# One PSUM bank moved from plain products to attention scores in a two-layer hybrid decoder

## Chip, cores and metric

The kernel runs on one core of one Trainium2 chip. The metric is the device time of one execution in microseconds (us), lower is better. Before the change three runs took 1982.52, 1983.05 and 1984.99 us; their median is 1983.05 us.

## What is computed

x has 512 tokens of 1024 channels in float32. Two layers run one after the other, each of this form (shortened from the reference):

```python
h = rms_norm(x, mix_norm_g[l])
proj = h @ w_in[l]                       # split into the inputs of three mixers and three gates
ya = nsa_mixer(...)      # compressed blocks, selected blocks, window: 8 heads of 64
yb = mla_mixer(...)      # latent attention: 8 heads, 96 wide keys, 64 wide values
yc = rglru_mixer(...)    # causal conv, gated linear recurrence, GeLU gate
merged = sigmoid(ma) * (ya @ w_pa[l]) + sigmoid(mb) * (yb @ w_pb[l]) + sigmoid(mc) * (yc @ w_pc[l])
x = x + merged @ w_o[l]
h = rms_norm(x, ffn_norm_g[l])
x = x + (silu(h @ ffn_w1[l]) * (h @ ffn_w3[l])) @ ffn_w2[l]
```

In `nsa_mixer` the compressed branch first makes one key and one value for every block of 32 tokens with a small two-layer network (`cmp_w1`, `cmp_w2`); with 512 tokens the selected branch selects all causal blocks, so both it and the window branch are causal attention.

## The kernel before

**Products.** Every large product is done in two halves per operand: `split` (L99) makes a high part on ScalarE (ACT, L100) and a low part on VectorE (DVE) or GpSimd (POOL) (L101), and `mm3` (L111) issues three matmuls (L113 to L115) per 128 rows of the contraction. A product of 1024 rows and 512 columns (`gemm_gen`, L121) is 24 matmuls into one PSUM tile of 128 x 512 float32, one bank. `block_tm` (L393) fills four banks at once, 24 matmuls each.

**PSUM.** `ps(tag)` (L87) takes a tile from one of four rotating sets of banks: `mm` for plain products, `s` for attention scores, `t` for transposes, `o` for the attention output. A tile's first matmul waits until the last reader of the tile that had its bank before is done. `pbufs` (L76) gives the number of banks of each set; together they are the eight banks. In the dense part (`wide`, L1219 on: the recurrence, the merges, the output product and the feed-forward network) a plain product takes its bank from `mm`, `s` and `t` in the order of the table `WIDE` (L33), seven banks in turn.

**Order.** The program is written in Python order by `layer` (L1078), and a list scheduler then orders the instructions of each engine with its own model of durations and free banks. So what is queued where follows from the banks too. Each engine runs its instructions in that order.

**A layer.** First the products for the compressed branch (`kv`, L1084, two tiles that stay open over eight steps) beside the first token-major block (L1085); then `b_in` (L757: five plain products with an eviction by DVE L339, a scaling by ACT L768 and DVE L769, and a square by ACT L774), of which the second is left open after two of its eight steps while `block3` (L404, evicted by ACT L413, L414, L422 and DVE L423) runs. Inside `block3` the two first stages of the compressed network (`cmp_mlp` L450; 16 small matmuls L461 each, evicted by ACT L465 and DVE L466) are put: the first takes a `t` bank, the second an `mm` bank (L459). Then the second token-major block, and the query and key transposes (`a_qk` L547: PE L544, ACT L551, DVE L550).

The attention (`attn`, L706) is a loop over 24 jobs of three stages each: scores (`st_s` L616: matmuls L748 and L749, or L113 to L115 for the latent heads; DVE L633 masks and finds the minimum in the bank; ACT L636 exponentiates out of the bank, which is then free), normalising (DVE L643, L645), transposes (`st_t` L649: PE L660, ACT L100, DVE L101) and values (`st_v` L666: L673, L674). Between them `fill` (L342) puts steps of plain products: the gate products (`gates_a` L930, evicted by DVE L339), the key-value products of the latent heads (`b_kv` L848: 16 per layer, six matmuls of 256 columns each, evicted by ACT L863, ACT L422 and DVE L423), their queries (`b_halfq` L807, ACT L819) and the first merge (`merge_a` L935, DVE L938).

Of the kernel before, what the change touches and what calls it, by code (L numbers as in the profile page):

```python
# [29 lines left out]
TLAG, VLAG = 6, 2  # L30
EB = 79
F0, F1 = 11.5, 2.5
WIDE = ("s", "t", "mm", "t", "s", "mm", "t")  # L33
YK, YQ = 1.3, 1.5
KB = 2
NLAG = 4, 4
# [27 lines left out]
class Builder:  # L64
    def __init__(self, ctx, tc, io, layers=L, dbg=None):
        self.tc, self.nc, self.io, self.layers = tc, tc.nc, io, layers
        self.dbg = dbg or {}
        nc = self.nc
        self.V, self.A, self.T = nc.vector, nc.scalar, nc.tensor
        pool = lambda n, b=1, **k: ctx.enter_context(tc.tile_pool(name=n, bufs=b, **k))  # L70
        self.cst, self.sb, self.sm = pool("cst"), pool("sb"), pool("sm", 2)
        self.psum = pool("psum", 1, space=PSUM)
        self.n = 0
        self.bufs = dict(wr=3, wh=4, wl=4, h=16, mg=8, oT=8, cq=10, qk=8, v=8, big=6, pt=5, P0=2, P1=2, P2=2, P3=3, e=3)
        self.pending = False
        self.pbufs = dict(mm=2, s=2, t=3, o=1)  # L76
        self.wide, self.turn = False, 0
        self.weng, self.debt, self.mid = None, 0.0, False

# [7 lines left out]
    def ps(self, tag="mm"):  # L87
        if tag == "mm" and self.wide:
            self.turn += 1
            tag = WIDE[self.turn % 7]  # L90
        return self.psum.tile([128, 512], F32, tag=tag, name=self.nm("ps" + tag), bufs=self.pbufs[tag])
# [986 lines left out]
    def layer(self, l):  # L1078
# [2 lines left out]
        self.wide, self.weng, self.peng = False, None, V  # L1081
        self.rows(l)
        self.bg = [self.rope_tables()] if l == 0 else []
        kv = [self.ps(), self.ps()]  # L1084
        for k in self.steps(self.block_tm(io["wb12"][l, 0], N12)):  # L1085
            if k % 4 == 0:
                w = [self.weights(self.win(l, c, 0)[:, k * 128:k * 128 + 512]) for c in ("kc", "vc")]
            s = slice((k % 4) * 128, (k % 4) * 128 + 128)
# [139 lines left out]
        for oc in range(KC):  # L1228
            t = self.pg("mg")
# [95 lines left out]
```

## Time and profile before

| what | us |
|---|---|
| median of three runs | 1983.05 |
| the profiled execution, its own time | 1982.81 |
| its span, first to last instruction | 1981.0 |
| TensorE matmul (PE) busy | 1935.6 |
| VectorE (DVE) busy | 1319.7 |
| ScalarE (ACT) busy | 996.6 |
| GpSimd (POOL) busy | 252.0 |

Layer 0 runs from 0 to about 1000 us, layer 1 from there to the end. In each layer the attention and what feeds it takes about the first 340 us, the dense part the rest. "Busy" is the union of an engine's instructions; for PE the ends are modelled and matmuls overlap, so that the distance from start to start tells a matmul's price better than its length. In a timeline row the bracket at the end is the idle time of the engine just before, and what ended it.

### The profile page before, as it was taken

The page shows a single profiled execution, that of the slowest core. Times are in us where ns is not written, and L with a number is a line of the kernel's source. Part 1 is how long each engine was busy: PE and PEld are TensorE (multiplying, and loading weights), DVE is VectorE, ACT ScalarE, POOL GpSimd, SP SyncE. Part 2 cuts the span into 40 slices and gives each one's busy share as a digit, 9 for nine tenths or more (in the row PEclk, how much of TensorE's full clock was granted, in tenths as well). Part 3 has the DMA queues.
Part 4 walks back from the last instruction along what each step waited for, and adds up shares of the span by engine and source line. Part 5 has one row for each costly group of instructions (what it writes and reads, how often), then busy time and mean ns, then how long its engine had stood idle before and what let it go on. Part 6 is the DMA issues. An engine that isn't in the chain of part 4 may idle for free.

```text
span 1981.0 us, 26967 instructions
## 1 busy us (share of the span) xinstructions
PE 1935.6 (98%) x9472; PEld 1627.8 (82%) x9472; DVE 1319.7 (67%) x2783; ACT 996.6 (50%) x1937; POOL 252.0 (13%) x232
## 2 busy tenths in 40 slices
PE   9898999999999999999999899999999999999999
PEld 8777878888888888888888688888888888888887
DVE  8689998788545554455556999878874465534542
ACT  5466776687334332233344577857773343323331
POOL 0453442000000000000004536310000000000000
PEclk9999999999999999999999999999999999999999
DMA  5211101223333223323432111113233322333333
GB/s 159 86 56 34 41 31 43 87 94 104 109 125 101 96 96 93 99 98 96 131 112 93 43 41 44 38 46 100 95 102 119 121 91 100 96 94 99 97 102 100
DMA packets 100519, 173.94 MB, mean 88 GB/s; under 512 B 11936, under 2 KB 26144, under 8 KB 100384
## 3 DMA queue, kind: packets, MB, share of 16 engines
q1 hardware_dynamic: 100384, 172.22, 27.3%
q8 instruction: 74, 1.21, 0.2%
q14 instruction: 61, 0.50, 0.1%
HBM read 167.98 MB, written 4.19 MB: 87 GB/s over the span
## 4 chain that ended last, share of the span: by engine, by line
PE 78%; DVE 8%; ACT 2%; issue 1%; POOL 0%; ACTq 0%; DVEq 0%; POOLq 0%
PE pst L114 9%; PE pst L113 9%; PE pst L115 9%; PE psmm L113 8%; PE psmm L114 8%; PE psmm L115 8%; PE pss L114 7%; PE pss L113 7%; PE pss L115 7%; PE pst L660 1%; DVE P L645 1%; DVE pss L633 1%; PE pso L673 1%; PE pso L674 1%; ACT P L636 1%
## 5 line engine op out<-in xcount | busy, mean ns | idle before, releaser
L100 ACT ACTIVATE wh<-wr 128x512 fp32r<-128x512 f32 (+3 forms) x640 | 387.5, 608 | 698.4 <-PE pst L114 261.0
L101 DVE TENSOR_TENSOR wl<-wr,wh 128x512 fp32r<-128x512 f32 (+2 forms) x526 | 355.1, 676 | 247.5 <-ACT wh L100 242.4
L101 POOL TENSOR_TENSOR wl<-wr,wh 128x512 fp32r<-128x512 f32 (+2 forms) x114 | 138.8, 1224 | 951.8 <-ACT wh L100 935.8
L113 PE MATMUL psmm<-h,wh 128*128 128x512 f32 x600 | 237.2, 395 | 3.7 <-ACT wh L100 2.8
L115 PE MATMUL psmm<-h,wl 128*128 128x512 f32 x600 | 235.2, 392 | 0.6 <-POOL wl L101 0.6
L114 PE MATMUL psmm<-h,wh 128*128 128x512 f32 x600 | 235.0, 392 | 0.0
L113 PE MATMUL pst<-h,wh 128*128 128x512 f32 x512 | 199.8, 390 | 0.0
L114 PE MATMUL pst<-h,wh 128*128 128x512 f32 x512 | 199.3, 389 | 0.0
L115 PE MATMUL pst<-h,wl 128*128 128x512 f32 x512 | 199.3, 389 | 0.0
L113 PEld LDWEIGHTS psmm<-h,wh 128*128 128x128 f32 x600 | 112.9, 188 | 26.4 <-ACT wh L100 3.2
L113 PE MATMUL pss<-h,wh 128*128 128x512 f32 x344 | 134.2, 390 | 0.0
L115 PE MATMUL pss<-h,wl 128*128 128x512 f32 x344 | 133.9, 389 | 0.0
L114 PE MATMUL pss<-h,wh 128*128 128x512 f32 x344 | 133.9, 389 | 0.0
L115 PEld LDWEIGHTS psmm<-h,wl 128*128 128x128 f32 x600 | 112.9, 188 | 24.6 <-POOL wl L101 1.1
L114 PEld LDWEIGHTS psmm<-h,wh 128*128 128x128 f32 x600 | 112.9, 188 | 20.8
L636 ACT ACTIVATE P<-pss,nm 128x512 f32<-128x512 f32 x192 | 100.1, 525 | 55.4 <-DVE nm L633 32.3
L113 PEld LDWEIGHTS pst<-h,wh 128*128 128x128 f32 x512 | 96.1, 188 | 20.2 <-ACT e L984 0.4
L115 PEld LDWEIGHTS pst<-h,wl 128*128 128x128 f32 x512 | 96.1, 188 | 20.1
L114 PEld LDWEIGHTS pst<-h,wh 128*128 128x128 f32 x512 | 96.1, 188 | 19.8
L633 DVE CUSTOM_DVE_ANT_0 pss<-pss,mask 128x512 f32<-128x512 f32 x192 | 93.7, 489 | 7.2 <-PE pss L115 5.8
L660 PE MATMUL pst<-ident,P 128*128 128x128 f32 x480 | 76.6, 274 | 11.5 <-DVE P L645 5.3
L660 PEld LDWEIGHTS pst<-ident,P 128*128 128x128 f32 x480 | 58.2, 141 | 28.1 <-issue 17.8
(423 smaller groups left out, 4303.4 us busy)
## 6 DMA issues: line engine op xcount, KB each, us to landing
wr<-w SPq DMA_DIRECT2D x240, 256.0 KB, 2.6
wr<-wfm SPq DMA_DIRECT2D x188, 256.0 KB, 2.6
wr<-wpc SPq DMA_DIRECT2D x32, 256.0 KB, 2.6
wr<-wo SPq DMA_DIRECT2D x32, 256.0 KB, 2.6
wr<-wb SPq DMA_DIRECT2D x32, 192.0 KB, 2.4
wr<-w SPq DMA_DIRECT2D x32, 192.0 KB, 2.3
mg<-xT SPq DMA_DIRECT2D x16, 256.0 KB, 2.7
wr<-wpa SPq DMA_DIRECT2D x16, 256.0 KB, 2.6
```

What stands on the lines that cost most here:

```text
L100: self.A.activation(hi, src, AF.Copy)
L101: (eng or self.V).tensor_tensor(lo, src, hi.bitcast(F32), OP.subtract)
L113: mm(ps, a[0], b[0], start=first, stop=False)
L114: mm(ps, a[0], b[1], start=False, stop=False)
L115: mm(ps, a[1], b[0], start=False, stop=last)
L633: self.V.tensor_tensor_reduce(p[:, :W], p[:, :W], self.mask[:, 512 - W:], 1.0, 3e38, OP.add, OP.min, j.nm[:, i:i + 1])
L636: self.A.activation(j.Pi[i], p[:, :128 * (i + 1)], AF.Exp, bias=j.nm[:, i:i + 1], scale=-1.0, accum_out=j.l[:, i:i + 1])
L645: V.tensor_scalar(j.Pi[i], j.Pi[i], j.gate[:, i:i + 1], j.l[:, i:i + 1], op0=OP.mult, op1=OP.mult)
L660: self.T.transpose(ps[:, c:c + 128], j.Pi[i][:, kt * 128:kt * 128 + 128], self.ident)
L673: T.matmul(o[:, 512 - n:], j.V[kt], h[:, m0:m0 + n], start=j.first and kt == 0, stop=False)
L674: T.matmul(o[:, 512 - n:], j.V[kt], l_[:, m0:m0 + n], start=False, stop=j.last and kt == NT - 1)
```

## The change

Three places: the banks become one for plain products, three for scores, three for transposes, one for the output; the table of the dense part visits those seven banks; and the second of the two open tiles at a layer's start comes from the score banks, as one `mm` bank can't hold two open tiles.

```diff
-WIDE = ("s", "t", "mm", "t", "s", "mm", "t")
+WIDE = ("s", "t", "mm", "s", "t", "s", "t")
...
-        self.pbufs = dict(mm=2, s=2, t=3, o=1)
+        self.pbufs = dict(mm=1, s=3, t=3, o=1)
...
-        kv = [self.ps(), self.ps()]
+        kv = [self.ps(), self.ps("s")]
```

No instruction is added or removed; 1464 of PE's 9323 matmuls stand at another place in its order, all of them before the dense parts or in their first steps.

**Place one, the start of layer 1.** On PE, before, the second product of the compressed network (L461 into `psmm_10121`) stands inside `block3`:

```order
L115 MATMUL pss_9970<-wh_10099,h_9463 128x312
L461 MATMUL psmm_10121<-pt_9876,qk_10117 64x62 x8
L461 MATMUL psmm_10121<-pt_9877,qk_10118 64x62 x8
L113 MATMUL pst_9967<-wh_10144,h_9523 128x312
L114 MATMUL pst_9967<-wl_10145,h_9523 128x312
```

Now it stands after the end of the open product of `b_in` (`psmm_9935`), whose bank it has to take over, and the third product of `b_in` (`psmm_10276`) stands behind it:

```order
L113 MATMUL pst_10290<-wh_10294,h_9159 128x384
L114 MATMUL pst_10290<-wl_10295,h_9159 128x384
L461 MATMUL psmm_10121<-pt_9876,qk_10117 64x62 x8
L461 MATMUL psmm_10121<-pt_9877,qk_10118 64x62 x8
L115 MATMUL pst_10290<-wh_10294,h_9160 128x384
L113 MATMUL pss_10291<-wh_10294,h_9159 128x384
L114 MATMUL pss_10291<-wl_10295,h_9159 128x384
L115 MATMUL pss_10291<-wh_10294,h_9160 128x384
L113 MATMUL pss_10292<-wh_10294,h_9159 128x384
L113 MATMUL psmm_10276<-h_9159,wh_10278 128x512
```

So 16 small matmuls moved from the middle of `block3` to a place some 40 matmuls later. On ACT, before, the eviction of that product (L465 from `psmm_10121`) stood ahead of those of `block3`:

```order
L100 ACTIVATE wh_10251<-wr_10250 128x512
L465 ACTIVATE cth_10138<-psmm_10121 64x62
L100 ACTIVATE wh_10278<-wr_10277 128x512
L422 ACTIVATE v_10184<-pst_9967,ny_9775 128x4x64
L422 ACTIVATE v_10189<-pst_9968,ny_9775 128x4x64
```

and now it stands behind the scaling and the square (L768, L774) of the product whose bank it follows:

```order
L100 ACTIVATE wh_10332<-wr_10331 128x384
L768 ACTIVATE cq_10270<-e_10268,vec_6780 128x512
L774 ACTIVATE e_10268<-e_10268 128x512
L465 ACTIVATE cth_10138<-psmm_10121 64x62
L100 ACTIVATE wh_10351<-wr_10350 128x384
```

On DVE L466 moves in the same way, behind the two additions L538. Layer 0 has the same move.

**Place two, the query and key transposes of layer 0.** On PE, before, the first of them (L544) stand inside the product after next:

```order
L113 MATMUL psmm_1185<-h_121,wh_1187 128x512
L114 MATMUL psmm_1185<-h_122,wh_1187 128x512
L115 MATMUL psmm_1185<-h_121,wl_1188 128x512
L544 MATMUL pst_1198<-ident,big_563 128x128 x2
L544 MATMUL pst_1198<-ident,big_564 128x128 x2
```

Now two sets stand at once behind the product `psmm_924`, while its bank is emptied:

```order
L115 MATMUL psmm_924<-h_169,wl_1116 128x512
L544 MATMUL pst_1198<-ident,big_563 128x128 x2
L544 MATMUL pst_1198<-ident,big_564 128x128 x2
L544 MATMUL pst_1233<-ident,big_563 128x128 x2
L544 MATMUL pst_1233<-ident,big_564 128x128 x2
L113 MATMUL psmm_1141<-h_79,wh_1143 128x512
```

The first set moved 30 matmuls of 512 columns ahead.

**Place three, the latent heads' key-value products of layer 0.** On PE, before, between two of them there was other work or a free second bank:

```order
L114 MATMUL psmm_2187<-wl_2142,cq_1252 128x256
L115 MATMUL psmm_2187<-wh_2141,cq_1253 128x256
L544 MATMUL pst_2208<-ident,big_1322 128x128 x2
L113 MATMUL psmm_2197<-wh_2141,cq_1180 128x256
L114 MATMUL psmm_2197<-wl_2142,cq_1180 128x256
```

Now three of them share the one bank with nothing, and with three transposes, between them:

```order
L114 MATMUL psmm_2146<-wl_2142,cq_1252 128x256
L115 MATMUL psmm_2146<-wh_2141,cq_1253 128x256
L113 MATMUL psmm_2187<-wh_2141,cq_1180 128x256
L114 MATMUL psmm_2187<-wl_2142,cq_1180 128x256
L115 MATMUL psmm_2187<-wh_2141,cq_1181 128x256
L113 MATMUL psmm_2187<-wh_2141,cq_1252 128x256
L114 MATMUL psmm_2187<-wl_2142,cq_1252 128x256
L115 MATMUL psmm_2187<-wh_2141,cq_1253 128x256
L660 MATMUL pst_2261<-ident,P_1951 128x128
L660 MATMUL pst_2261<-ident,P_1952 128x128
L660 MATMUL pst_2261<-ident,P_1953 128x128
L113 MATMUL psmm_2197<-wh_2141,cq_1180 128x256
```

Most of the other key-value products have 9 to 16 matmuls of other work between them now.

## Rows read from the trace of the kernel before

**Rows 1.** The page's first lines: span, and PE's busy time, share and instructions.

```profile
span 1981.0 us, 26967 instructions
PE 1935.6 (98%) x9472; PEld 1627.8 (82%) x9472; DVE 1319.7 (67%) x2783; ACT 996.6 (50%) x1937; POOL 252.0 (13%) x232
```

**Rows 2.** Waits of PE, longest in total: engine line, released by: us, times, longest.

```profile
PE pss L748 <- ACT P L636: 10.6, 13, 1.4
PE pst L660 <- DVE P L645: 5.3, 3, 2.7
```

**Rows 3.** Busy us by stretch: length, PE, PEld, DVE, ACT, POOL, granted clock, DMA.

```profile
65.00:85.00 20.00, 12.98 (x56) 10.75 (x56) 16.00 (x42) 9.69 (x25) 10.25 (x7) 0.91 0.17 49
85.00:105.00 20.00, 20.00 (x104) 18.04 (x103) 3.20 (x5) 9.64 (x17) 10.98 (x10) 1.00 0.41 129
105.00:300.00 195.00, 176.93 (x1043) 149.64 (x1041) 187.18 (x554) 136.90 (x359) 84.36 (x79) 0.99 0.13 39
...
340.00:1000.00 660.00, 659.61 (x2924) 546.15 (x2924) 386.44 (x602) 291.23 (x458) 2.27 (x2) 1.00 0.32 103
1055.00:1085.00 30.00, 28.47 (x150) 25.39 (x148) 12.50 (x25) 14.37 (x33) 13.68 (x13) 1.00 0.32 101
1085.00:1145.00 60.00, 51.77 (x273) 41.24 (x271) 57.18 (x172) 32.83 (x81) 34.08 (x27) 0.97 0.14 45
1145.00:1275.00 130.00, 126.59 (x782) 110.43 (x781) 121.06 (x376) 104.09 (x276) 53.48 (x54) 1.00 0.13 40
```

**Rows 4.** Timeline of PE at the start of layer 1: start, length, instruction.

```profile
1048.56 2.08 PE L461 MATMUL psmm<-pt,qk 128*64 128x62 f32 x32
...
1057.94 0.39 PE L115 MATMUL psmm<-h,wl 128*128 128x512 f32 x1
...
1061.16 0.44 PE L114 MATMUL pst<-wl,h 128*128 128x384 f32 x1 [0.54 <-POOL wl L101]
...
1062.74 0.44 PE L113 MATMUL pss<-wh,h 128*128 128x384 f32 x1
...
1068.37 0.44 PE L114 MATMUL pst<-wl,h 128*128 128x384 f32 x1 [0.50 <-POOL wl L101]
```

**Rows 5.** Timelines of DVE, then ACT, at the same place.

```profile
1058.47 0.20 DVE L466 SCALAR_TENSOR_TENSOR chid<-cth,psmm 64x62 f32<-64x62 f32 x1
...
1063.01 0.68 DVE L339 TENSOR_TENSOR e<-psmm,rsb 128x512 f32<-128x512 f32 x1
...
1065.83 1.01 DVE L538 TENSOR_TENSOR big<-big,e 128x384 f32<-128x384 f32 x2
...
1065.94 0.63 ACT L774 ACTIVATE e<-e 128x512 f32<-128x512 f32 x1 [1.49 <-DVE cq L769]
```

**Rows 6.** Timeline of PE at the start of layer 0.

```profile
74.34 0.66 PE L113 MATMUL pss<-wh,h 128*128 128x384 f32 x1 [0.31 <-ACT kpe L414]
...
77.69 0.40 PE L114 MATMUL pst<-wl,h 128*128 128x384 f32 x1
...
81.25 0.34 PE L113 MATMUL pst<-wh,h 128*128 128x384 f32 x1
83.18 0.44 PE L114 MATMUL pst<-wl,h 128*128 128x384 f32 x1 [1.60 <-POOL wl L101]
```

**Rows 7.** Timeline of ACT at the same place in layer 0.

```profile
78.70 0.63 ACT L774 ACTIVATE e<-e 128x512 f32<-128x512 f32 x1 [1.26 <-DVE cq L769]
```

**Rows 8.** Groups of DVE by shape, 85 to 340 us: count, busy us, mean ns, idle.

```profile
L423 DVE SCALAR_TENSOR_TENSOR v<-psmm,bbckvy,v 128x128 fp32r<-128x128 f32 x16 | 5.5, 345 | 0.8 <-ACT v L422 0.4
L339 DVE TENSOR_TENSOR mg<-psmm,rsb 128x512 f32<-128x512 f32 x8 | 5.4, 679 | 0.0
```

**Rows 9.** One key-value product of layer 1: its last matmul, and its bank's last reader.

```profile
1164.06 0.28 PE L115 MATMUL psmm<-wh,cq 128*128 128x256 f32 x1
...
1166.01 0.35 DVE L423 SCALAR_TENSOR_TENSOR v<-psmm,bbckvy,v 128x128 fp32r<-128x128 f32 x1
```

## The prediction

> **What bounds the kernel now.** I read the page's first lines, then the waits of PE, then the busy time by stretch. The first shows that PE is busy for 1935.6 of 1981.0 us [rows 1]: 45 us of idle time at most can be won without leaving out matmuls. The list of waits shows where a score bank is short: 13 times, 10.6 us in all, the first matmul of a score tile (L748) waits for ACT's exponential (L636), the bank's last reader [rows 2]. This is the wait that a third score bank aims at. The stretches show where it can matter. In the dense part (340 to 1000 us) PE is busy for 659.6 of 660 us; nothing can be won there. In the attention of layer 0 (105 to 300 us) PE is idle 18.1 us, but DVE only 195 − 187.2 = 7.8 us: DVE is the bound there, and PE's waits are mostly its shadow. At the start of layer 1's attention (1085 to 1145 us) DVE is idle 2.8 of 60 us. In the rest of it (1145 to 1275 us) PE is idle only 3.4 us, DVE 8.9: there PE is the bound [rows 3]. So freer scores can win at most 7.8 + 2.8 + 3.4 = 14 us.
>
> **The dense parts: nothing.** The new table also visits seven banks in turn, so each bank comes back after seven products as before. A product that is left in its bank for six others has no wait before, and none now. SP's order of loads is the same throughout, so no transfer waits behind another.
>
> **A. The starts of the layers (place one): +7.8 us.** With one plain bank the compressed network's second product (L461) can't start before the open product of `b_in` is finished and evicted, and `b_in`'s third product can't start before L465 and L466 have read that.
>
> Layer 1. The 32 matmuls that start at 1048.56 us take 2.08 us; without them the open product's last matmul (1057.94 us) ends its work some 2 us earlier. What follows does not gain that: the next block's first matmuls wait for evictions and for POOL (0.54 us at 1061.16); I count 0.3 us [rows 4]. L339, which empties the bank, starts at 1063.01 and takes 0.68 us, so with the 0.3 us off it ends at 1063.4. The 32 small matmuls then run till 1065.5, five matmuls of 384 columns (0.87 us) till 1066.4. The third product waits for L465, now behind ACT's square, which ends at 1065.94 + 0.63 − 0.3 = 1066.3, and for L466 (0.20 us), behind the two additions L538 at 1065.83 on DVE: 1066.9 us [rows 5]. Six more matmuls (1.36 us) bring PE to 1068.25 at a point that it passed at about 1063.0: 5.2 us late. The POOL wait of 0.50 us at 1068.37 falls away, so 4.7 us stay.
>
> The clock comes on top. [...]
>
> Layer 0 has the same move. There the square ends at 78.70 + 0.63 = 79.3 [rows 7], L465 and L466 at 79.8, six matmuls at 81.2, where PE was at 78.1: 3.1 us late. The POOL wait of 1.60 us at 83.18 [rows 6] takes up half: +1.5. In sum 4.7 + 1.6 + 1.5 = 7.8; between 0, if the list order hides it, and 5.2 + 1.6 + 3.1 = 9.9.
>
> **B. The third score bank: −4 us.** All 13 waits should go, 10.6 us. But where DVE is the bound, a score that is ready earlier only waits longer for L633. I take −4, under half, because most of the waits lie where DVE has almost no idle time left. Bounds: 0 and −10.6.
>
> **C. Layer 0's transposes 30 matmuls earlier (place two): −4 us.** From 85 to 105 us PE is full and DVE idle for 16.8 of 20 us [rows 3]; after that DVE is the bound. Thirty matmuls of 512 columns at 0.227 us are 6.8 us, by which the attention can begin earlier; of this the 1.5 us by which A is late go off, and a little for the weights that the displaced product needs. Bounds: 0 and −6.8. B and C share the ceiling of 14.
>
> **D. One plain bank within the attention (place three): +7 us.** Each layer has 16 key-value products of six matmuls; each holds its bank until DVE's L423 (0.345 us) has read it, and the eight gate products until L339 (0.68 us) has [rows 8]. One instance in layer 1: last matmul at 1164.06 + 0.28, L423 ends at 1166.01 + 0.35, so the bank stands 2.0 us after its product [rows 9]. In the new order most of these products have 9 to 16 matmuls of other work between them, some 1.6 us by their columns, and at two places per layer little or nothing. PE is then short of 0.5 us at 14 places and of 1.8 us at two: 10.6 us a layer. In layer 0 DVE is the bound, and PE's wait for a plain bank costs nothing as long as scores are ahead; should DVE run dry, the cover is gone. In layer 1 PE is the bound; of 10.6 us the 3.4 us that PE stands idle there anyway [rows 3] go off: +7. The trace has no wait for a single plain bank, so the bounds are wide: 0, if the eviction keeps up, and 37, if both layers pay (21.2) and the 16 gate products about 1 us each.
>
> **Sum.** The profiled execution took 1982.81 us (its span is 1981.0; it is 0.24 below the median). 1982.81 + 7.8 − 4 − 4 + 7 = 1989.6 us, or 0.34% more. No change can be told from a difference within 0.2%, some 4 us: 1979 to 1987.
>
> **The rivals.**
>
> *Faster: the attention is what counts.* If DVE stays fed, B and C reach their ceiling together and D is hidden: 1982.81 + 7.8 − 14 = 1976.6 us. For it speaks that the 13 waits are PE's largest group in the attention, against it that DVE has 4% of idle time there. It decides if DVE's idle time from 105 to 300 us falls below about 2 us. Chance 0.24.
>
> *No change: the second plain bank was worth nothing.* D is 0, as a product's eviction needs three short instructions on two engines, and the scheduler puts other work between. A, B and C alone give 1982.81 + 7.8 − 8 = 1982.6 us. Against it speaks the bank that stands 2.0 us against some 1.6 us of other work [rows 9]. [...] Chance 0.20.
>
> *Much slower: the waits bring the clock down.* If D is some 30 us, since both layers pay and PE pauses at each of some 48 products, the time is 1982.81 − 0.2 + 30 = 2012.6 us. For it speaks that the granted clock is already 0.97 from 1085 to 1145 us and 0.99 from 105 to 300, where PE waits most [rows 3], against it that in layer 0 the pauses lie beside a full DVE. [...] No run here shows yet that a bank alone does it. It decides if the granted clock from 1145 to 1275 us falls below 0.95. Chance 0.11.
>
> **How the numbers follow.** The forecast, 1987 to 2003 us, gets 0.45: A rests on rows instruction by instruction, B and C on an idle time that bounds them, D on a lag of which one instance was read. Slower by over 0.2% are the forecast and the heavy case, 0.45 + 0.11 = 0.56; within it 0.20; faster 0.24. The range has to hold most of the fast rival, whose own time is 1976.6, and a part of the heavy one: 1975 to 2006 us.
>
> **What would show it.** In the profile after the change:
> - A: PE waits for `chid` L466 or ACT L465 near 1065 us and near 80 us, and the POOL waits behind them are gone; the granted clock just after 1066 us is under 1.
> - B: the waits of L748 for ACT are gone. If the time between 105 and 300 us is the same none the less, DVE was the bound.
> - C: the first score tiles of layer 0 come up to 5 us earlier, and DVE's idle time in 85 to 105 us is shorter.
> - D: waits of plain products (`psmm`, L113) for DVE L423, L339 or ACT, 10 us and more, with those of layer 1 in its PE-bound stretch.
> - The dense parts have the same length as before.
>
> The forecast is wrong if A's late start is caught up later (the layers would then reach their dense parts as early as before), or if D's waits don't show in layer 1.

## The result, and the profile after

The changed kernel takes 2011.03 us (median of 4 runs, 2009.52 to 2011.94), beside 1984.01 us for the kernel before, measured with it: a ratio of 1.0130, 95% interval 1.0117 to 1.0142 (the quotient of these two medians, 1.0136, lies inside it). It is 27 us slower; the forecast was 1989.6. The profiled execution took 2010.46 us.

The page's first lines of the changed kernel (span; busy us of each engine):

```profile
span 2008.7 us, 26938 instructions
PE 1951.3 (97%) x9472; PEld 1642.1 (82%) x9472; DVE 1320.2 (66%) x2783; ACT 998.6 (50%) x1937; POOL 250.9 (12%) x232
```

The span grew by 27.7 us. Beside [rows 1] that splits in two: PE is idle for 2008.7 − 1951.3 = 57.4 us instead of 45.4, which is 12.0 us more, and it is busy 15.7 us longer **with the same 9472 matmuls**. Of the second part my sum had 1.6 us, in A. Matmuls ran at a lower clock: the mean granted clock of the run is 0.986, where it was 0.997. As an estimate that is enough for it: 0.011 of 2008.7 us is 22 us at full clock, a part of which fell into PE's pauses.

Waits of PE in the changed kernel (engine line, released by: us in total, times, longest):

```profile
PE pst L113 <- ACT wh L100: 10.4, 3, 5.9
PE psmm L113 <- DVE mg L339: 8.6, 5, 2.3
PE pst L660 <- DVE qk L550: 4.5, 2, 2.7
PE psmm L113 <- DVE v L423: 4.0, 4, 1.3
...
PE pss L748 <- ACT P L636: 1.7, 2, 1.3
...
PE psmm L461 <- DVE e L339: 1.2, 1, 1.2
...
PE psmm L113 <- DVE chid L466: 0.8, 1, 0.8
```

The waits of scores for ACT have gone from 10.6 us [rows 2] to 1.7: the third score bank does what it should. In their place stand waits of plain products (`psmm`) for the one plain bank, most of all for L339, the eviction of the gate products.

Busy us by stretch (length, PE, its weight loads PEld, DVE, ACT, POOL, granted clock, DMA), to be read beside [rows 3]:

```profile
65.00:85.00 20.00, 12.44 (x75) 10.62 (x76) 17.20 (x48) 8.10 (x22) 8.03 (x5) 0.83 0.10 31
85.00:105.00 20.00, 20.00 (x107) 18.27 (x106) 3.41 (x5) 10.79 (x19) 10.79 (x10) 1.00 0.39 125
105.00:300.00 195.00, 177.19 (x1015) 151.71 (x1015) 175.81 (x532) 132.19 (x344) 80.19 (x75) 0.95 0.12 38
...
340.00:1000.00 660.00, 659.69 (x2943) 546.51 (x2942) 389.95 (x613) 296.54 (x470) 2.59 (x2) 1.00 0.31 101
...
1055.00:1085.00 30.00, 24.48 (x145) 22.29 (x144) 19.54 (x37) 9.36 (x25) 10.44 (x11) 0.89 0.23 70
1085.00:1145.00 60.00, 53.99 (x284) 45.20 (x284) 46.06 (x128) 35.42 (x80) 33.16 (x26) 0.98 0.21 70
1145.00:1275.00 130.00, 122.17 (x691) 106.33 (x691) 115.73 (x357) 87.58 (x229) 55.07 (x55) 0.93 0.13 40
```

From 105 to 300 us the granted clock fell from 0.99 to 0.95, from 1145 to 1275 us from 1.00 to 0.93. DVE, which bounded the first of these stretches with 187.2 of 195 us, is now busy for 175.8: it runs dry behind PE. The dense part is as full as before.

Where the time is lost can be followed by four marks: the first score matmul (L748) of each layer, and the first convolution of the recurrence (L969, on DVE), which opens each layer's dense part.

| mark | before, us | after, us | late by |
|---|---|---|---|
| layer 0, first L748 | 113.11 | 107.32 | −5.8 |
| layer 0, first L969 | 352.14 | 362.03 | 9.9 |
| layer 1, first L748 | 1088.74 | 1104.74 | 16.0 |
| layer 1, first L969 | 1329.78 | 1357.80 | 28.0 |

Busy us between these marks (columns as above), first of the kernel before, then of the changed one:

```profile
0.00:113.11 113.11, 103.48 (x576) 92.46 (x577) 83.52 (x248) 60.45 (x115) 33.27 (x33) 0.98 0.38 119
113.11:352.14 239.03, 220.90 (x1311) 188.72 (x1310) 221.11 (x633) 164.81 (x428) 93.50 (x86) 0.99 0.12 38
352.14:1088.74 736.60, 734.68 (x3377) 615.00 (x3376) 430.13 (x694) 326.85 (x531) 26.18 (x24) 1.00 0.32 103
1088.74:1329.78 241.04, 229.07 (x1353) 196.03 (x1352) 217.25 (x639) 169.62 (x435) 99.03 (x90) 0.99 0.14 42
```

```profile
0.00:107.32 107.32, 95.49 (x541) 85.58 (x541) 80.83 (x242) 56.94 (x109) 30.95 (x31) 0.97 0.38 118
107.32:362.03 254.71, 234.97 (x1346) 201.03 (x1347) 220.36 (x639) 169.26 (x434) 96.55 (x89) 0.96 0.12 39
362.03:1104.74 742.71, 736.95 (x3377) 617.29 (x3376) 430.62 (x695) 329.00 (x532) 24.78 (x23) 1.00 0.32 102
1104.74:1357.80 253.06, 236.75 (x1353) 202.47 (x1352) 220.57 (x639) 168.40 (x434) 98.62 (x90) 0.96 0.13 40
```

The attention of layer 0 begins 5.8 us early and ends 9.9 late. It is 15.7 us longer from mark to mark, but these are not all lost: ahead of the first score PE now does 35 matmuls fewer (541 for 576, 8.0 us of busy time), and has them to do behind it. Lost up to the dense part of layer 0 are 9.9 us, the start of layer 1 costs 6.1 us, its attention 12.0. The dense parts cost nothing.

| up to the mark | PE idle longer by, us | PE busy longer by, us |
|---|---|---|
| layer 0, first L969 (from 0) | 3.8 | 6.1 |
| layer 1, first L748 | 3.8 | 2.3 |
| layer 1, first L969 | 4.3 | 7.7 |

The matmuls of each of these stretches are the same in number. So in the two stretches that hold the attentions (the first row and the last) the longer matmuls cost more than the pauses: 13.8 us against 8.1.

**The start of layer 1.** Timelines of the changed kernel, PE first (start, length, instruction, idle before it and what ended it):

```profile
1065.48 0.39 PE L115 MATMUL psmm<-h,wl 128*128 128x512 f32 x1
1069.54 0.45 PE L113 MATMUL pst<-wh,h 128*128 128x384 f32 x1 [3.67 <-ACT wh L100]
...
1073.22 3.67 PE L461 MATMUL psmm<-pt,qk 128*64 128x62 f32 x32 [1.21 <-DVE e L339]
```

Then DVE, and ACT:

```profile
1067.41 0.96 DVE L532 TENSOR_TENSOR big<-big,cosa 128x768 f32<-128x768 f32 x1
1068.28 0.87 DVE L423 SCALAR_TENSOR_TENSOR v<-pst,ny,v 128x256 fp32r<-128x256 f32 x2
```

```profile
1068.80 0.28 ACT L413 ACTIVATE gth<-pst,ny 128x24 f32<-128x24 f32 x1 [6.92 <-DVE v L423]
1068.98 0.51 ACT L100 ACTIVATE wh<-wr 128x384 fp32r<-128x384 f32 x1
```

The wait for L339 ahead of L461 is the one that I had worked out. The larger one, 3.67 us, I had not (layer 0 has its like, 5.91 us at 69.52 us, where the longest was 2.81 before): PE stands before weights that ACT's L100 has to make, L100 stands behind L413, L413 waits for L423, and DVE does L532 first. Before the change PE spent that time on the third product of `b_in` and had needed no more than 0.54 us at that place [rows 4]. With one plain bank that product can't start, so the cover is gone. The 32 small matmuls (the trace has two for each of the program's 16), 2.08 us before [rows 4] at a granted clock of 1.00, take 3.67 at one of 0.50.

**The attention.** Three of PE's pauses in the changed kernel:

```profile
145.15 0.39 PE L674 MATMUL pso<-z,v 128*128 128x256 f32 x1 [2.29 <-DVE z L101]
...
148.71 0.80 PE L113 MATMUL psmm<-h,wh 128*128 128x512 f32 x1 [1.72 <-DVE mg L339]
...
167.29 0.79 PE L113 MATMUL psmm<-h,wh 128*128 128x512 f32 x1 [2.33 <-DVE mg L339]
```

and what DVE does ahead of the second:

```profile
146.17 0.68 DVE L101 TENSOR_TENSOR pt<-pst,pt 128x512 fp32r<-128x512 f32 x1
146.77 0.67 DVE L605 TENSOR_TENSOR e<-e,cl 128x496 f32<-128x496 f32 x1
147.35 0.69 DVE L633 CUSTOM_DVE_ANT_0 pss<-pss,mask 128x512 f32<-128x512 f32 x1
...
147.96 0.69 DVE L339 TENSOR_TENSOR mg<-psmm,rsb 128x512 f32<-128x512 f32 x1
```

The last matmul of the gate product before it starts at 142.00 us; L339 empties its bank at 148.65. For more than 6 us the only plain bank is full, because DVE has its queue of attention work ahead of L339. PE comes to the next gate product, stops, and with it stop the scores behind it in its order (after the wait of 1.72 us that ends at 148.71 the next L748 starts at 151.71). DVE then runs out of scores. The matmuls right after such a pause are long (0.80 us of 512 columns, where the groups of the page show 0.39). The granted clock is 0.50 from 145.9 to 152.8 us and from 166.4 to 173.2, which is 3.4 us of clock lost each time; the first of these falls begins ahead of the wait that ends at 148.71, the second inside the one that ends at 167.29.

**The lead of 5.8 us.** It comes from the 35 matmuls that stand behind the first score now, and it melts as they are done and as PE waits for the plain bank (1.74 us for L339 at 124.31): the seventh L748 is 1.8 us early (121.62 us, 123.37 before), the ninth 2.7 late (132.56, before 129.91). DVE's order changed here as well. DVE, then POOL, in the changed kernel:

```profile
141.35 0.81 DVE L788 TENSOR_TENSOR e<-kpe 128x128 f32<-128x128 f32 x1 [3.37 <-POOL big L538]
```

```profile
140.31 1.01 POOL L538 TENSOR_TENSOR big<-big,e 128x384 f32<-128x384 f32 x1
```

In the kernel before, L788 stands at 151.25 us in DVE's order and has no gap; POOL's first L538 of this chain stands at 142.54. L788 came forward by 9.9 us and POOL's work by 2.2 only, so DVE waits 3.37 us for it. The L101 for which PE waits 2.29 us at 145.15 stands behind this in DVE's order. So this pause of PE is one of the new order and not a wait for the plain bank.

### The profile page after: what moved, and what is told of

It reads as the page before. It is cut to its first block, busy times and chain, and to the rows that moved or that the text cites. A ratio compares the mean times of both kernels' runs of the same rounds, so it can differ in the third digit from the quotient of the medians.

```text
span 2008.7 us, 26938 instructions
## 1 busy us (share of the span) xinstructions
PE 1951.3 (97%) x9472; PEld 1642.1 (82%) x9472; DVE 1320.2 (66%) x2783; ACT 998.6 (50%) x1937; POOL 250.9 (12%) x232
## 4 chain that ended last, share of the span: by engine, by line
PE 83%; DVE 13%; ACT 2%; issue 1%; POOL 1%; DMA 0%; SPq 0%; DVEq 0%; ACTq 0%
PE pss L114 10%; PE pss L113 10%; PE pss L115 10%; PE pst L115 10%; PE pst L114 10%; PE pst L113 10%; PE psmm L113 6%; PE psmm L115 5%; PE psmm L114 5%; PE pst L660 2%; DVE P L645 2%; DVE pss L633 1%; PE pso L674 1%; PE pso L673 1%; PE pst L544 1%
## 5 line engine op out<-in xcount | busy, mean ns | idle before, releaser
L100 ACT ACTIVATE wh<-wr 128x512 fp32r<-128x512 f32 (+3 forms) x640 | 388.3, 609 | 712.6 <-PE pst L114 256.2
L101 DVE TENSOR_TENSOR wl<-wr,wh 128x512 fp32r<-128x512 f32 (+2 forms) x526 | 354.6, 675 | 244.7 <-ACT wh L100 241.6
L101 POOL TENSOR_TENSOR wl<-wr,wh 128x512 fp32r<-128x512 f32 (+2 forms) x114 | 138.6, 1220 | 950.3 <-ACT wh L100 941.9
L113 PE MATMUL pss<-h,wh 128*128 128x512 f32 x536 | 208.8, 390 | 0.0
L115 PE MATMUL pss<-h,wl 128*128 128x512 f32 x536 | 208.7, 389 | 0.0
L114 PE MATMUL pss<-h,wh 128*128 128x512 f32 x536 | 208.6, 389 | 0.0
L113 PE MATMUL pst<-h,wh 128*128 128x512 f32 x528 | 205.9, 390 | 0.0
L114 PE MATMUL pst<-h,wh 128*128 128x512 f32 x528 | 205.4, 389 | 0.0
L113 PE MATMUL psmm<-h,wh 128*128 128x512 f32 x392 | 158.2, 404 | 10.3 <-DVE mg L339 8.6
L115 PE MATMUL psmm<-h,wl 128*128 128x512 f32 x392 | 155.2, 396 | 0.0
L114 PE MATMUL psmm<-h,wh 128*128 128x512 f32 x392 | 155.2, 396 | 0.0
L636 ACT ACTIVATE P<-pss,nm 128x512 f32<-128x512 f32 (+1 forms) x192 | 100.1, 525 | 61.2 <-DVE nm L633 30.4
L114 PEld LDWEIGHTS pss<-h,wh 128*128 128x128 f32 x536 | 100.6, 188 | 21.0
L113 PEld LDWEIGHTS pss<-h,wh 128*128 128x128 f32 x536 | 100.6, 188 | 20.8
L115 PEld LDWEIGHTS pss<-h,wl 128*128 128x128 f32 x536 | 100.6, 188 | 20.8
L113 PEld LDWEIGHTS pst<-h,wh 128*128 128x128 f32 x528 | 99.1, 188 | 20.3
L633 DVE CUSTOM_DVE_ANT_0 pss<-pss,mask 128x512 f32<-128x512 f32 (+1 forms) x192 | 94.0, 490 | 13.2 <-PE pss L749 6.6
L113 PEld LDWEIGHTS psmm<-h,wh 128*128 128x128 f32 x392 | 74.9, 191 | 27.5 <-DVE mg L339 10.8
```

What stands on the lines that cost most here:

```text
L100: self.A.activation(hi, src, AF.Copy)
L101: (eng or self.V).tensor_tensor(lo, src, hi.bitcast(F32), OP.subtract)
L113: mm(ps, a[0], b[0], start=first, stop=False)
L114: mm(ps, a[0], b[1], start=False, stop=False)
L115: mm(ps, a[1], b[0], start=False, stop=last)
L633: self.V.tensor_tensor_reduce(p[:, :W], p[:, :W], self.mask[:, 512 - W:], 1.0, 3e38, OP.add, OP.min, j.nm[:, i:i + 1])
```

## The experiments

All ratios are to the kernel before, run on the same chip; the changed kernel's is 1.0130. "Clock" is the mean granted clock, "idle" the span less PE's busy time, both of the profiled execution; that is one of several, and executions of one kernel differ by some 4 us (the kernel before from 1982.67 to 1986.56 beside all_s; the profiled one of cmp_s was the longest of four, 2010.69 at a median of 2006.55). PE's busy time is that of 9472 matmuls, 9538 in the last row.

| kernel | ratio, 95% interval | PE busy, us | idle, us | clock |
|---|---|---|---|---|
| before | 1 | 1935.6 | 45.4 | 0.997 |
| changed | 1.0130, 1.0117 to 1.0142 | 1951.3 | 57.4 | 0.986 |
| cmp_s | 1.0108, 1.0093 to 1.0123 | 1953.4 | 55.5 | 0.987 |
| mgprio | 1.0115, 1.0099 to 1.0131 | 1950.1 | 55.2 | 0.988 |
| gates_s | 1.0114, 1.0097 to 1.0131 | 1947.3 | 57.6 | 0.992 |
| bkv_s | 1.0106, 1.0091 to 1.0121 | 1950.4 | 53.6 | 0.989 |
| undo_a | 1.0098, 1.0084 to 1.0112 | 1947.9 | 53.1 | 0.991 |
| mm1_s2 | 1.0150, 1.0136 to 1.0164 | 1954.9 | 57.0 | 0.985 |
| mm2_s3_t2 | 1.0033, 1.0021 to 1.0046 | 1942.7 | 46.4 | 0.993 |
| shared4 | 1.0043, 1.0030 to 1.0055 | 1942.3 | 49.2 | 0.992 |
| all_s | 1.0040, 1.0028 to 1.0052 | 1947.6 | 43.5 | 0.994 |
| mm2_s3_t2_fix | 0.9999, 0.9990 to 1.0008 | 1938.8 | 44.1 | 0.995 |
| before_mgprio | 1.0015, 1.0006 to 1.0024 | 1939.8 | 45.9 | 0.995 |
| fill | 1.0110, 1.0093 to 1.0127 | 1960.9 | 44.8 | 0.993 |

**One part alone: cmp_s, mgprio, gates_s, bkv_s.** Each is the changed kernel with one edit.

```diff
# cmp_s
-            ps = self.ps("mm" if z else "t")
+            ps = self.ps("s" if z else "t")
# mgprio
-        tm = self.rs_mul(ps, tag)
+        with self.tc.high_priority(offset=WPRI if tag == "mg" else 0):
+            tm = self.rs_mul(ps, tag)
# gates_s
-        ps = yield from self.gemm_gen(self.win(l, nme, oc), self.h)
+        ps = yield from self.gemm_gen(self.win(l, nme, oc), self.h, "s" if nme == "ma" else "mm")
# bkv_s, in b_kv
-            ps = self.ps()
+            ps = self.ps("s")
```

> The changed kernel with the compressed network's second product in a score bank: place one undone, the attention's order nearly untouched. Theory 1 (the displaced product costs what the traces show at the layers' starts, 1.8 us in layer 0 and 6.2 in layer 1): 8 us under the changed kernel, about 2003. Rival (it costs nothing in the end, all 27 us arise in the attention): within 3 us of 2011. If PE still pauses near 65 us of layer 0 for ACT's weights, the pause belongs to ACT's sine, not to the bank.

> The changed kernel with the gate products' evictions L339 given priority: three of layer 0 stand up to eight instructions earlier on DVE, nothing else of weight moves. Theory 2 (PE stands at the one plain bank for L339, 1.72 us at 148.7 and 2.33 us at 167.3, and each pause is followed by 3.4 us of lost clock): some 2 us of idle time go, and with the two falls of the clock about 6 to 8 us in all, 2003 to 2006. Rival A (idle alone counts, the clock falls anyway): 2009. Rival B (DVE is the bound in layer 0, so its order is worth nothing): 2011 within 2 us.

> The changed kernel with the eight gate products of a layer in score banks. Theory 2 (the five waits for L339, 8.6 us, and the falls of the clock that follow them are half or more of the loss): 1993 to 2002, though score tiles may wait again, at most the 10.6 us of before. Rival (the key-value products cost it, not the gates): 2008 to 2014. Rival (any third user of the score banks only moves the waits): 2011 or more, with waits of L748 or L113 for ACT P of 8 us or more.

> The changed kernel with the 16 key-value products of a layer in score banks. Theory 3 (their waits for L423, 4.0 us, the waits of 1.8 and 2.7 us behind them at 197.7 and 1188.8, and the clock after them cost 8 to 12 us): 1999 to 2003. Rival (gates cost it, the key-value products are hidden): within 3 us of 2011.

All four are 3 to 5 us faster than the changed kernel (0.0015 to 0.0024 of 1984), less than the theories asked for, and no two can be told apart at intervals of ±0.0015; mgprio and gates_s can't be told from the changed kernel either. cmp_s missed its 8 us for a reason that I had overlooked: the third product of `b_in` still waits for the one plain bank. gates_s shows the trade: the waits for L339 fell from 8.6 to 1.8 us and those of scores for ACT came back to 8.9, with the same idle time. Its clock is higher all the same (0.992), so the sum of the pauses alone doesn't set the clock. mgprio took the waits for L339 from 8.6 to 6.0 us only. No single user of the plain bank makes the loss.

**Place one undone whole: undo_a.** cmp_s, and the third product as well:

```diff
-                ps = yield from self.gemm_gen(self.win(l, nme, c), self.h, "t" if t0 else "mm")
+                ps = yield from self.gemm_gen(self.win(l, nme, c), self.h, "t" if t0 else "s" if (nme, c) == ("bcq", 2) else "mm")
```

> The changed kernel with place one undone whole: the compressed network's second product and the third product of the latent inputs both in score banks, so that neither waits for the open product's bank. Theory 1 (the layers' starts cost 1.8 + 6.2 us, and the attention costs the rest): 8 us under the changed kernel, a ratio of 1.009 to the kernel before (the changed kernel: 1.013). Rival (a late start is caught up later): 1.012 to 1.013. Rival (the start is most of it, as a late start also upsets the attention): under 1.005.

1.0098: 0.0032 or 6.4 us under the changed kernel, as theory 1 has it within the interval. PE's busy time from 1055 to 1085 us is back at 28.52 us (28.47 before [rows 3]) and the clock there at 1.00. The edit does more than its name says: the list scheduler put layer 0's transposes back too (first L544 at 105.01 us, 99.41 in the changed kernel, 104.44 before), so place two is undone with it. By the marks the start of layer 1 takes 736.4 us again (736.6 before, 742.7 changed), layer 0 reaches its dense part 6.2 us late instead of 9.9, without the lead, and the attention of layer 1 is 2.3 us longer than in the changed kernel. The attention costs the rest, some 19 us, also with an undisturbed start.

**The banks apart: mm1_s2 and mm2_s3_t2.** Seven banks, and another eight:

```diff
# mm1_s2, from the changed kernel
-        self.pbufs = dict(mm=1, s=3, t=3, o=1)
+        self.pbufs = dict(mm=1, s=2, t=3, o=1)
-        kv = [self.ps(), self.ps("s")]
+        kv = [self.ps(), self.ps("t")]
# mm2_s3_t2, from the kernel before
-        self.pbufs = dict(mm=2, s=2, t=3, o=1)
+        self.pbufs = dict(mm=2, s=3, t=2, o=1)
-            ps = self.ps("mm" if z else "t")
+            ps = self.ps("mm" if z else "s")
```

(with tables for the dense part that visit the banks there are).

> Seven banks: one plain, two for scores, three for transposes, one for the output; the eighth is unused. It takes the plain bank away and gives nothing for it. Theory (the plain bank makes the loss, the third score bank pays a little): 1.013 to 1.020, with the waits of L748 for ACT of 8 us or more back and those of plain products kept. Rival (the third score bank upsets the order and makes the loss): 1.000 to 1.006.

> Two plain banks, three for scores, two for transposes: the third score bank is paid for with a transpose bank. Theory (the plain bank makes the loss): no waits for L339, waits of transposes instead, 0.998 to 1.008. Rival (the score waits were what bounds the attention): 0.993 to 0.997, faster than the kernel before. Rival (a third score bank itself makes the loss): 1.010 or more.

Two of the waits of mm1_s2, then two of mm2_s3_t2:

```profile
PE pss L748 <- ACT P L636: 7.7, 9, 1.8
...
PE psmm L113 <- DVE mg L339: 4.1, 3, 1.6
```

```profile
PE pst L660 <- DVE pt L101: 12.5, 8, 3.7
PE pst L113 <- DVE e L339: 7.8, 2, 3.9
```

This is the pair that decides. Taking the second plain bank away and giving nothing for it costs 0.0150; giving the third score bank then returns 0.0020, 4 us, with intervals that overlap. Buying the third score bank with a transpose bank costs 0.0033 in all. The plain bank makes the loss; the third score bank may be worth the 4 us that I had taken for it, which the intervals (4 ± 3.7 us) hardly tell from nothing. The waits of scores for ACT came back, 7.7 us where 8 were foretold, but those for L339 halved from 8.6 to 4.1 us, and the kernel is no faster for it: the waits for L339 alone don't measure the loss.

**Sharing: shared4 and all_s.** shared4 has four banks for plain products and scores in common; all_s is undo_a, gates_s and bkv_s together.

```diff
# shared4, from the kernel before
-        self.pbufs = dict(mm=2, s=2, t=3, o=1)
+        self.pbufs = dict(s=4, t=3, o=1)
+        elif tag == "mm":
+            tag = "s"
```

> Four banks in turn for plain products and scores together, three for transposes. Theory (PE stands because one bank has to be emptied by DVE before the next plain product): a bank comes back only after three other tiles, so the waits for L339 fall under 3 us and the clock from 1145 to 1275 us is 0.97 or more, 0.996 to 1.004. Rival (in a common rotation scores wait for the slow gate products instead): 1.006 or more, with waits for L339 or ACT P over 10 us.

> The changed kernel with place one undone whole and both the gate products and the key-value products in score banks: only the latent queries and the first merge still share the one plain bank. If the three parts add up as measured alone (0.0032 for the starts, 0.0016 for the gates, 0.0024 for the key-value products): 1.006. Theory (each alone leaves the other's pauses, which keep the clock down; together they go): 1.002 to 1.005, mean granted clock 0.993 or more. Rival (the order of the list scheduler and not the bank): 1.008 or more.

shared4 gave 1.0043, at the edge of its theory, with the clock at 1.00 from 1145 to 1275 us (0.96 from 105 to 300); its longest waits are of transposes. all_s gave 1.0040: 18 us better than the changed kernel, where the parts measured alone add up to 14. The difference of 4 us is no more than the intervals allow. So the theory of pauses that support each other is not shown by it, but most of the loss does go when the plain products leave the one bank. What is left of it is not idle time, of which there is less than before (43.5 us against 45.4): PE is busy 12.0 us longer. A clock of 0.994 instead of 0.997 makes some 6 us of that; what makes the rest stays open.

**The third score bank made to fit: mm2_s3_t2_fix.** The two waits of 3.9 us above taken away:

```diff
# from mm2_s3_t2
-            ps = self.ps("mm" if z else "s")
+            ps = self.ps("mm" if z else "o")
-                ps = yield from self.gemm_gen(self.win(l, nme, c), self.h, "t" if t0 else "mm")
+                ps = yield from self.gemm_gen(self.win(l, nme, c), self.h, "s" if t0 else "mm")
```

> Two plain, three score, two transpose banks, with the first latent product moved from a transpose bank to a score bank and the compressed network's first product to the output bank. The two waits of 3.9 us for L339 at the layers' starts go: 7.8 us, from 1.0033 to about 0.999 to 1.000. If the third score bank pays in the attention as well: 0.996 to 0.998. Rival (the waits move to the next user of the banks): 1.002 or more.

0.9999: the waits went and 6.7 us with them. It equals the kernel before and doesn't beat it.

**A control: before_mgprio.** The edit of mgprio in the kernel before.

> The kernel before with the gate products' evictions given priority on DVE. With two plain banks PE never waits for L339 in the attention, so the theory expects no change, 0.999 to 1.001; a gain of 0.002 or more would say that DVE's order matters by itself and not through the plain bank.

It was 0.0015 slower, where no change was expected. Priority for a few evictions moved about a hundred of DVE's 2783 instructions in the trace, some thirty of ACT's and about a hundred places in PE's order, and that cost 3 us with no bank involved. Effects of that size, those of the four single parts among them, can come from the order alone.

**The pauses filled: fill.** Into mm1_s2, with the unused eighth bank `x`; `FILL` names eight tiles by number and gives each 6 to 10 matmuls:

```diff
+        if self.n in FILL:
+            x = self.psum.tile([128, 512], F32, tag="x", name=f"psx{self.n}", bufs=1)
+            for _ in range(FILL[self.n]):
+                self.T.matmul(x, self.h[0][0][:, :128], self.h[0][0], start=True, stop=True)
```

> The seven-bank kernel (ratio 1.0150, granted clock 0.985) with 66 matmuls of 512 columns into the unused bank, whose result nobody reads, put ahead of the eight products and transposes at which PE paused longest: 15 us more PE work at 0.227 us each. Theory (the pauses bring the clock down, and the clock is over half of the loss): the matmuls run in the pauses, the granted clock rises to 0.989 or more, and with more work the kernel is no slower, 1.009 to 1.015. Rival (the loss is the waiting itself, the clock falls for another reason): the clock stays at 0.985 and the time stays or grows, 1.015 to 1.022.

The page's first lines of mm1_s2, then of fill:

```profile
span 2011.9 us, 26968 instructions
PE 1954.9 (97%) x9472; PEld 1643.9 (82%) x9472; DVE 1319.1 (66%) x2783; ACT 998.7 (50%) x1937; POOL 250.9 (12%) x232
```

```profile
span 2005.7 us, 27092 instructions
PE 1960.9 (98%) x9538; PEld 1645.1 (82%) x9538; DVE 1322.4 (66%) x2783; ACT 997.7 (50%) x1937; POOL 250.2 (12%) x232
```

and the attention of mm1_s2, then of fill, by stretch (columns as above):

```profile
105.00:300.00 195.00, 177.97 (x1004) 150.84 (x1002) 172.18 (x522) 131.56 (x340) 80.93 (x75) 0.95 0.12 37
...
1085.00:1145.00 60.00, 55.30 (x288) 46.92 (x286) 42.18 (x118) 33.26 (x74) 32.97 (x26) 0.97 0.21 68
1145.00:1275.00 130.00, 119.65 (x678) 103.05 (x679) 116.06 (x357) 88.19 (x229) 57.10 (x56) 0.95 0.13 43
```

```profile
105.00:300.00 195.00, 183.28 (x1060) 153.33 (x1058) 179.06 (x543) 134.69 (x351) 83.37 (x78) 0.99 0.12 38
...
1085.00:1145.00 60.00, 56.46 (x300) 46.78 (x299) 49.03 (x138) 35.73 (x81) 31.69 (x27) 1.00 0.20 66
1145.00:1275.00 130.00, 123.33 (x716) 104.80 (x715) 116.17 (x351) 89.90 (x235) 54.53 (x54) 0.99 0.13 39
```

With 66 useless matmuls the kernel is 0.0040, 8 us, faster, outside the rival's range and with intervals that don't meet. Idle time fell by 57.0 − 44.8 = 12.2 us, and PE's busy time rose by 6.0 where 66 × 0.227 = 15.0 us of work was added (0.227 us is the step from one 512-column matmul to the next that the prediction uses, and that the kernel before has on average over the 28 steps from 599.64 to 605.99 us; the trace gives the 66 as a group 19.5 us, ends overlapping): the old matmuls took some 9 us less. The clock came back to 0.99 and 1.00 in all three stretches of the attention. So the lower clock follows from the pauses, and its price is real. The fill also let the scheduler move other instructions, and a part of the gain of order size (3 us) could be that. A part of the clock's return is: from 145 to 155 us it is at 1.00 (0.68 in mm1_s2), though no added matmul starts between 115 and 160 us; the pause of 2.30 us that stood there is gone. The whole return is larger than the order's effect in the control: 0.985 to 0.993 here, 0.997 to 0.995 there. Of the waits, those for L339 hardly changed (4.1 to 3.7 us).

## Why the prediction was wrong

**Step A, the layers' starts, held, in its number better than in its parts.** Foretold +7.8. Layer 1 measured 16.0 − 9.9 = 6.1 against 4.7 + 1.6 = 6.3, and undo_a gives back 6.4 ± 3.7 us, with place two undone as well. L461 did wait for L339, which ended when I had it (1073.17 us; 1063.4 foretold, and the layer began 9.9 later). But the third product didn't wait for L466 behind it, as foretold (L466 ended at 1077.39, PE came to the product at 1078.23). The pauses grew by 3.8 us where I had 4.7, the busy time by 2.3 where I had 1.6 for the clock (0.89 from 1055 to 1085 us, 1.00 before), and the largest pause was one that I left out, for ACT's weights, bare because the product that had covered it couldn't run. No run shows the term of 1.6 us; in its place the changed kernel's trace shows a granted clock of 0.50 from 1071.0 to 1077.8 us, which is 3.4 us of clock lost, with PE busy 2.3 us longer. In layer 0 the first L544 came 5.0 us early instead of the 6.8 of its 30 matmuls: 1.8 us by that, where 1.5 were foretold.

**Step B, the third score bank, is not shown either way.** Foretold −4 between 0 and −10.6. The waits went, from 10.6 to 1.7 us. mm1_s2 against the changed kernel gives −4 ± 3.7, but of the 3.2 us between their traces 1.3 lie ahead of the first score, where no score bank counts.

**Step C, the earlier transposes of layer 0, came and brought nothing that the runs show.** The first score came 5.8 us early. I had counted the 30 matmuls that the transposes passed as won for the attention, but PE has to do them behind the first score. The lead pays only if they fit into PE's idle time in the attention, and that did not shrink (18.1 us between the marks before, 19.7 after). By the ninth score tile the lead was a lag. undo_a gives the lead up, and its layer 0 reaches the dense part 3.7 us earlier. That DVE would have less idle time from 85 to 105 us was wrong too (16.6 us; 16.8 before).

**Step D, one plain bank within the attention, is the one that failed.** I had +7 with bounds of 0 and 37. By the marks layer 0 lost 9.9 us, some 1.8 of them at its start, and the attention of layer 1 12.0; undo_a leaves some 19 us over the kernel before, the gains of B, if any, included. D is thus about 20 us, or 23 if B gave its 4. Three of its parts were wrong.

- *The wrong users.* I priced 32 key-value products by a lag of 2.0 us, read from one instance [rows 9]. They waited four times, 4.0 us (twice before, 1.2 us). The gate products, which I had put into the upper bound at about 1 us each, waited five times, 8.6 us; one bank stood full for more than 6 us, since L339 had DVE's queue ahead of it. The trace [rows 8] gave L339's own 0.68 us, and I took that for its lag. The sum of the pauses I did not undercount: PE's idle time in the attention of layer 1 grew by 4.3 us, where I had 7. What I undercounted are the next two.
- *Layer 0 counted as free.* "PE's wait for a plain bank costs nothing as long as scores are ahead." No scores were: PE works in order, so a pause at a gate product holds the scores behind it. DVE's idle time from 105 to 300 us went from 7.8 to 19.2 us.
- *The clock was left out of the attention.* I charged it at the layers' starts only. It fell to 0.95 and 0.93 in the two long stretches, and matmuls alone took 15.7 us more in the whole kernel, 13.8 of them by the marks in layer 0 up to its dense part and in the attention of layer 1.

**The rival that came true** was "much slower: the waits bring the clock down", 2012.6 us against 2011.0 measured, with 0.11 of the chance. Its sign to watch, a clock under 0.95 from 1145 to 1275 us, came at 0.93. fill supports the link that it rested on: with matmuls put into the pauses the granted clock went from 0.985 to 0.993. That its number fits so closely is luck: it had PE pause at each of some 48 products, and PE paused at nine of them, for L339 and L423. Most matmuls are as short as ever (L113 into `pss` with 512 columns has a mean of 390 ns before and after), and the whole is slower. The rival by which the second plain bank was worth nothing did not come true: without it mm1_s2 is 0.0150 slower.

That D was bounded at 37 us was right, and the value inside the bounds was taken from the cheapest user. The forecast's range, too, cut the heavy rival off.

What stays open: how the 20-odd us of D divide among gates, key-value products, queries and merges. Each alone gave back 3 to 5 us, which is little more than the order's own 3 us. Open too is how much of it is the new order of the instructions, which the scheduler makes for the banks, and how much the waiting for a bank itself: the pause behind L788 is of the first kind.

## What to carry to other kernels

A set of buffers with one member made the producer wait here for the consumer's whole queue (the bank stood full for more than 6 us), not for the consumer's instruction (L339, 0.68 us). So price the loss of a second buffer by the time from the producer's last write to the end of the eviction, at the worst user, and look at what stands behind the waiting instruction on its in-order engine. On TensorE add the clock that the pauses cost; PE's longer busy time, for which the lower clock is enough by the estimate above, was more than half of this loss (15.7 of 27.7 us). When work is brought forward, ask when the work that it passes gets done, and check that the other engines' chains that meet it come forward too.

## What the runs showed that I had not expected

- Useless work can pay: 66 matmuls put into pauses made mm1_s2 8 us faster, with PE busy 6.0 us longer.
- The same 9472 matmuls had PE busy between 1935.6 and 1954.9 us, with no other change than their order and banks (one execution of each kernel).
- Moving about a hundred DVE instructions of a tuned order cost 0.0015, with no wait for a bank added.
